# A gated ConvFFN on one core: three plain pairs before the Strassen pairs, the gated activations in smaller DRAM tensors, down loads in program order, one norm chain for the first rows

## The chip, the core and the metric

One core of a Trainium2 chip runs the whole kernel. The metric is the device time in microseconds (us) of one execution, as the median of several runs. Beside it stands one profiled execution, whose trace gives start and duration of the instructions on each engine: PE (TensorE, with PEld for its weight loads), DVE (VectorE), ACT (ScalarE), POOL (GpSimd) and SP (SyncE, here only a queue that issues DMAs).

## The reference

A decoder block on 1024 tokens of width 1024: a mixer (pooling and indexed sparse attention), then a channel mixer, then a last RMSNorm. The change touches only the channel mixer and the last norm:

```python
def conv_ffn(xn, w_up, conv_w, conv_b, w_down):
    h = xn @ w_up                                  # (1024, 1024) @ (1024, 5632)
    h = causal_depthwise_conv3(h, conv_w) + conv_b # over tokens, per channel
    a, b = jnp.split(h, 2, axis=-1)                # 2816 and 2816 channels
    return (jax.nn.silu(a) * b) @ w_down           # (1024, 2816) @ (2816, 1024)

h = h + conv_ffn(rmsnorm(h, norm_ffn_g), w_up, conv_w, conv_b, w_down)
out = rmsnorm(h, norm_final_g)
```

## The kernel before

All large products are taken at near-float32 precision: each operand is split in a high half (a cast to float32r on ACT) and a low half (the difference, on DVE or POOL), and three matmuls of 128x128 by 128x512 are issued for each pair of blocks, high by high, high by low and low by high (`mm3`, lines 85 to 87). A "step" of three such matmuls covers 128 of the contraction.

**Order of the work.** The program is built with a scheduler that keeps dependences and places instructions on each engine by its own model; inside `manual_schedule` the engines named keep program order. PE is in program order in both stages below. A tile pool hands out buffers by tag; when a pool is closed its addresses go to the next pool, and the first use of a buffer waits for the last use of the tiles that lay there.

**Up stage (`ffn_up`).** The normed input lies feature-major in `x2T`, as four blocks X[k, t] (k half of the features, t half of the tokens), X[k, 0] in two 16 KB tiles on the right side of SBUF and X[0, 1], X[1, 1] in the 16 KB tiles `x2T1a` and `x2T1b` on the left. The 5632 columns of `w_up` are taken as 22 pairs c = 0..21: 128 channels of a with the same 128 of b (o = 0, 1). `load(c)` brings the two weight blocks into one of two landing tiles `upr` of tag `raw`. Seven tiles of tag `op` hold split weights.

A plain pair (`plain`, c = 0 only) splits four weight blocks (o, k), the low halves of o = 0 on DVE and of o = 1 on POOL, and makes eight products of 12 matmuls each (96 matmuls), in the order (t, o) = (0,0), (0,1), (1,0), (1,1). A Strassen pair (`pair`, c = 1..21) treats weights and X as 2x2 blocks and makes seven products (84 matmuls), in the order of operands 1, 5, 2, 6, 7, 3, 4. It needs sums of weights (`combined`, on POOL, for c = 1 on DVE) and four sums of X, T1 to T4, each split and kept in a 16 KB tile on the right. They are made once, between the plain pair and pair 1, by 56 DVE operations of 128x512 with 16 ACT casts between; `t2f`, which carries a sum from the first half of that work to the last, takes one of the two landing tiles of tag `raw` while it lives.

`gated(c, H)` then makes the convolution (two operations on DVE for each of a and b, after one on ACT), silu on ACT, the product on POOL, and stores it by POOL's queue to a DRAM tensor `gd`. Accumulators and H have one buffer each.

**Down stage (`ffn_down`).** The product is again one Strassen step over halves of tokens, of the 2816 channels (f) and of the output (d). The 11 blocks of 128 channels in each half are taken in six groups j of two (the last of one). For a group, `prepare_*` loads quarters of `gd` and of `w_down` into landing tiles `raw` (512 KB each), makes sums, and splits them into an operand tile `op` (four of them). The order is: product 1 and 5 (`prepare_1_5`, five loads a group, in the order A(0,0), B(0,0), A(1,0), A(1,1), B(0,1)), then 2, 6 and 7, 3, 4. Each product is 24 matmuls a group. In product 4 the last three groups are kept and run token block by token block, so that rows finish one after the other. `cs`, `ct` keep the sums of products 1 and 5 for later; `h` (tile `hr`) takes the residual by four loads `load_h`.

**Last norm.** `row_done(th, tb, ...)` makes for one block of 128 rows the reciprocal root (`rstd`, ten DVE operations on 128x1), scales the two halves (ACT and DVE) and stores them. It is called for rows 0 to 3 before product 4 and for rows 4 to 7 at the end.

The pools of the down stage: on the right `hr` 32 KB, `gfin` 4 KB, `cs` and `ct` 22 KB each, `u2`, `u4` 8 KB each and small tiles (2.4 KB), where T1 to T4 and X[k, 0] lay before; on the left the four operand tiles (64 KB) and then ten landing tiles (40 KB).

Of the kernel before, what the change touches and what calls it, by code (L numbers as in the profile page):

```python
# [18 lines left out]
P = 128  # L19
D = 1024  # L20
# [19 lines left out]
class K:  # L40
# [4 lines left out]
    def split(self, src, hi, lo, eng=None, first=None):  # L45

        if first:
            first.tensor_copy(hi, src)
        else:
            self.nc.scalar.copy(hi, src)  # L50
        (eng or self.nc.vector).tensor_tensor(lo, src, hi.bitcast(F32), op=ALU.subtract)  # L51

    def rstd(self, pool, ssum, name, n=1, halves=False):


        nc = self.nc
        v, y, t, u = (pool.tile([P, n], F32, tag=f"rs_{c}{n}", name=name + c) for c in "vytu")
        if halves:
            nc.vector.tensor_scalar(v, ssum[:, 0:1], ssum[:, 1:2], EPS, op0=ALU.add, op1=ALU.add)
# [124 lines left out]
    def stages(self):  # L184
# [81 lines left out]
        self.gd = dram("gd", [2, 2, P, NFH, HB])  # L266
# [707 lines left out]
    def ffn_up(self, fw, pool, x2_last, close_h):  # L974
# [23 lines left out]
        def gated(c, H):  # L998
# [12 lines left out]
            nc.gpsimd.dma_start(self.gd[c // NFH, :, :, c % NFH].rearrange("t p c -> p t c"),  # L1011
# [48 lines left out]
        for k in range(4):  # L1060
            f = difference(1, k, xk((0, 1), k), xk((0, 0), k))
            keep(1, k, f)
            less(t2[:, k], xk((1, 1), k), f)
            keep(2, k, t2[:, k])
        for k in range(4):
            keep(3, k, difference(3, k, xk((1, 1), k), xk((0, 1), k)))
        for k in range(4):
            f = pool.tile([P, HB], F32, tag="s4", name=f"tf4_{k}")
            less(f, xk((1, 0), k), t2[:, k])
            keep(4, k, f)  # L1070
        T = {n: [t[:, 0], t[:, 1]] for n, t in T.items()}

        def pair(c):
# [23 lines left out]
            operand_of(4, A[1, 1], nc.gpsimd if c > 1 else nc.vector)  # L1097
# [19 lines left out]
        with self.tc.manual_schedule(engines=PE):  # L1117
            for c in range(1, NF):
                pair(c)

    def ffn_down(self, ring, pool):
# [3 lines left out]
        G, W = self.gd, io["w_down"]  # L1125
        h = pool.tile([P, NB, D], F32, name="hr")
# [4 lines left out]
        groups = [(j, min(2, NFH - j)) for j in range(0, NFH, 2)]  # L1131

        def quarters(j, n):


            def load(src, name):
                t = ring.tile([P, 2, HB], F32, tag="raw", name=f"raw{name}_{j}", bufs=10)[:, 0:n]
                nc.sync.dma_start(t, src[:, j:j + n])
                return t
            return (lambda t, f: load(G[f, t], f"g{t}{f}")), (lambda f, d: load(W[f, d], f"w{f}{d}"))  # L1140

        def operand(p, j, n):
            return ring.tile([P, 4, 2, HB], F32R, tag="op", name=f"op{p}_{j}", bufs=4)[:, :, 0:n]

        def put(t, side, val):
            self.split(val, t[:, 2 * side], t[:, 2 * side + 1])
# [23 lines left out]
        def prepare_6_7(j, n):  # L1170
            A, B = quarters(j, n)
            s, t = cs[:, j:j + n], ct[:, j:j + n]
# [8 lines left out]
        def prepare_3(j, n):  # L1181
            A, B = quarters(j, n)
            p3, a = operand(3, j, n), A(0, 1)
            put(p3, 0, combined(a, a, cs[:, j:j + n], sub))
# [3 lines left out]
        def prepare_4(j, n):  # L1188
            A, B = quarters(j, n)
            p4 = operand(4, j, n)  # L1190
            put(p4, 0, A(1, 1))
            b = B(1, 0)
            put(p4, 1, combined(b, b, ct[:, j:j + n], sub))
            return p4,

# [6 lines left out]
        def run(prepare, pss, fresh, tail=0):  # L1202

            kept = []
            for k, (j, n) in enumerate(groups):
                ts = prepare(j, n)
# [21 lines left out]
        ss = {}  # L1228

        def half_done(th, dh, tb):  # L1230

            b = 4 * th + tb
            if b not in ss:
                ss[b] = pool.tile([P, 2], F32, tag="ss", name=f"ssf{b}", bufs=8)
            junk = pool.tile([P, HB], BF16, tag="junk", name=f"sqf{b}{dh}", bufs=2)
            nc.scalar.activation(junk, quarter(th, dh, tb), AF.Square, scale=D ** -0.5, accum_out=ss[b][:, dh:dh + 1])
# [5 lines left out]
        def row_done(th, tb, scaled):  # L1242

            b = 4 * th + tb
            y = self.rstd(pool, ss[b], f"f{b}", halves=True)
            for dh in (1 - scaled, scaled):
                q, cols = quarter(th, dh, tb), slice(dh * HB, (dh + 1) * HB)
                if dh == scaled:
                    nc.scalar.activation(q, q, AF.Copy, scale=y)
                else:  # L1250
                    nc.vector.scalar_tensor_tensor(q, q, y, gfin[:, cols], op0=ALU.mult, op1=ALU.mult)
                nc.sync.dma_start(io["out"][b * P:(b + 1) * P, cols], q)

        with self.tc.manual_schedule(engines={mybir.EngineType.PE}):
# [35 lines left out]
            for tb in range(4):  # L1290
                q = quarter(0, 1, tb)
                tt(q, y[tb], q, op=add)
                half_done(0, 1, tb)
                row_done(0, tb, 0)
            run(prepare_4, (x,), False, 3)
            for tb in range(4):
# [3 lines left out]
                row_done(1, tb, 1)  # L1300
# [69 lines left out]
```

## Time and profile before

| | |
|---|---|
| median of 3 runs | 1536.83 us (1533.32 to 1537.8) |
| profiled execution, own time | 1532.94 us |
| span of the profiled execution (first to last instruction) | 1530.8 us |
| mean granted TensorE clock, share of full speed | 0.974 |
| PE busy | 1431.6 us, 94% |
| DVE busy | 1177.1 us, 77% |
| ACT, POOL busy | 652.7 us, 491.8 us |

Starts are in us from the start of the span. A row of a timeline gives start, duration, engine, line, operation, output and inputs, shapes and a count; in square brackets, the idle time of the engine before it and what ended it. Durations of pipelined matmuls are modelled, so the distance of their starts is the better measure.

### The profile page before, as it was taken

The numbers are of one execution on the slowest core, as the hardware profiler recorded it, in microseconds if no ns is written. First come the engines' busy times: TensorE is split into PE (matmuls) and PEld (weight loads), VectorE is DVE, ScalarE is ACT, GpSimd is POOL, SyncE is SP. The second block draws the span as 40 slices with busy tenths as digits, with TensorE's granted clock in tenths as the row PEclk, the third lists the DMA queues.
The fourth block names the chain that finished last, engine by engine and source line by source line (L and its number), as shares of the span: only waits on it lengthen the run. The fifth ranks groups of instructions, "written<-read, shape, count | busy, mean of one in ns | idle before, by whom it ended". The sixth has DMA issues, their size and how long they took to land.

```text
span 1530.8 us, 18757 instructions
## 1 busy us (share of the span) xinstructions
PE 1431.6 (94%) x6658; PEld 1173.2 (77%) x6658; DVE 1177.1 (77%) x1960; ACT 652.7 (43%) x1119; POOL 491.8 (32%) x359
## 2 busy tenths in 40 slices
PE   5999999999889899998999499999999997999996
PEld 4888887787678788986887378888888885788885
DVE  7756999999971356878357988888888885859697
ACT  7665322213332456864023434444444443444343
POOL 4102433213433364444100555555555541000000
PEclk9999999999999999999999699999999999999998
DMA  9002422412115466228412022222222215966452
GB/s 339 10 21 86 140 81 100 139 69 62 42 68 194 139 189 181 64 86 267 150 66 103 28 83 83 83 83 83 83 83 83 82 57 192 377 203 210 151 151 110
DMA packets 74062, 184.47 MB, mean 121 GB/s; under 512 B 8560, under 2 KB 13552, under 8 KB 73456
## 3 DMA queue, kind: packets, MB, share of 16 engines
q1 hardware_dynamic: 65360, 159.16, 30.2%
q0 software_dynamic: 8608, 24.12, 4.9%
q8 instruction: 52, 0.85, 0.2%
q14 instruction: 42, 0.34, 0.1%
HBM read 140.25 MB, written 40.89 MB: 118 GB/s over the span
## 4 chain that ended last, share of the span: by engine, by line
PE 64%; DVE 26%; DMA 3%; issue 3%; ACT 3%; POOL 1%; SPq 0%; DVEq 0%; ACTq 0%; POOLq 0%
DVE tk_junk L554 11%; PE up L85 9%; PE up L86 9%; PE up L87 9%; PE d L86 4%; PE d L87 4%; PE d L85 4%; PE o L835 2%; PE pt L818 2%; DVE tk_r L566 2%; DVE tk_cand L567 1%; PE is L439 1%; PE is L440 1%; PE wvp L86 1%; PE wvp L85 1%
## 5 line engine op out<-in xcount | busy, mean ns | idle before, releaser
L554 DVE TENSOR_SCALAR_CACHE_REDUCE tk_junk<-score,tk_cand 128x384 bf16<-128x384 f32 (+1 forms) x186 | 175.0, 941 | 1.8
L85 PE MATMUL up<-T,w 128*128 128x512 f32 x336 | 134.0, 399 | 20.3 <-ACT w L995 20.3
L1005 DVE SCALAR_TENSOR_TENSOR acc<-H,cw,acc 128x1023 f32<-128x1023 f32 x88 | 130.7, 1503 | 15.8 <-ACT acc L1003 14.9
L87 PE MATMUL up<-T,w 128*128 128x512 f32 x336 | 134.0, 399 | 1.1 <-DVE w L996 1.1
L86 PE MATMUL up<-T,w 128*128 128x512 f32 x336 | 133.8, 398 | 0.0
L85 PE MATMUL d<-op 128*128 128x512 f32 x308 | 121.4, 394 | 11.6 <-ACT op L50 11.6
L86 PE MATMUL d<-op 128*128 128x512 f32 x308 | 121.3, 394 | 1.3 <-DVE op L51 1.3
L87 PE MATMUL d<-op 128*128 128x512 f32 x308 | 120.8, 392 | 0.0
L1010 POOL TENSOR_TENSOR acc<-acc,acc 128x1024 f32<-128x1024 f32 x22 | 79.1, 3593 | 120.5 <-ACT w L995 70.8
L995 ACT CAST w<-s 128x512 fp32r<-128x512 f32 x84 | 52.1, 621 | 142.1 <-POOL s L1086 75.7
L996 DVE TENSOR_TENSOR w<-s,w 128x512 fp32r<-128x512 f32 x84 | 104.1, 1240 | 2.2 <-ACT w L995 1.3
L85 PEld LDWEIGHTS up<-T,w 128*128 128x128 f32 x336 | 63.6, 189 | 36.0 <-ACT w L995 20.8
L85 PEld LDWEIGHTS d<-op 128*128 128x128 f32 x308 | 58.5, 190 | 24.5 <-ACT op L50 12.4
L87 PEld LDWEIGHTS up<-T,w 128*128 128x128 f32 x336 | 63.6, 189 | 17.3 <-DVE w L996 1.9
L85 PE MATMUL up<-x2T,w 128*128 128x512 f32 x184 | 74.4, 405 | 2.3 <-ACT w L995 2.3
L86 PEld LDWEIGHTS up<-T,w 128*128 128x128 f32 x336 | 63.7, 190 | 15.2
L87 PE MATMUL up<-x2T,w 128*128 128x512 f32 x184 | 74.1, 403 | 0.0
L86 PE MATMUL up<-x2T,w 128*128 128x512 f32 x184 | 74.1, 402 | 0.0
L825 DVE TENSOR_TENSOR PT<-pt,PT 128x512 fp32r<-128x512 f32 (+3 forms) x96 | 50.5, 554 | 29.9 <-ACT PT L824 29.4
L996 POOL TENSOR_TENSOR w<-upr,w 128x512 fp32r<-128x512 f32 x22 | 34.6, 1574 | 112.5 <-DVE w L996 89.8
L1003 ACT ACTIVATE acc<-H,cb,cw 128x1024 f32<-128x1024 f32 x44 | 54.8, 1246 | 35.6 <-DVE H L1114 24.4
L86 PEld LDWEIGHTS d<-op 128*128 128x128 f32 x308 | 58.6, 190 | 14.4 <-DVE op L51 2.1
(871 smaller groups left out, 4097.4 us busy)
## 6 DMA issues: line engine op xcount, KB each, us to landing
upr<-w_up SPq DMA_DIRECT2D x44, 512.0 KB, 4.1
rawg<-gd SPq DMA_DIRECT2D x40, 512.0 KB, 4.9
raww<-w_down SPq DMA_DIRECT2D x35, 512.0 KB, 4.8
gd<-acc POOLq DMA_DIRECT2D x22, 512.0 KB, 3.2
g<-gt SPq DMA_DIRECT2D x32, 256.0 KB, 2.0
xb<-x SPq DMA_DIRECT2D x8, 512.0 KB, 5.6
xTr<-xT SPq DMA_DIRECT2D x8, 512.0 KB, 6.4
mixd<-mixed SPq DMA_DIRECT2D x16, 256.0 KB, 2.6
```

The costliest lines, as they stand in the source:

```text
L85: t.matmul(ps, sh, mh, start=start, stop=False, skip_group_check=onto)
L86: t.matmul(ps, sh, ml, start=False, stop=False, skip_group_check=onto)
L87: t.matmul(ps, sl, mh, start=False, stop=stop, skip_group_check=onto)
L554: nc.vector.tensor_scalar(junk[:, :W], self.score[b], thr, None, op0=ALU.is_ge, op1=ALU.add, accum_out=cnt[:, j:j + 1])
L566: nc.vector.tensor_scalar(r, cnt, float(TOPK), float(1 << bit), op0=ALU.is_lt, op1=ALU.mult)
L818: nc.tensor.transpose(pt[:, j - j0, :], t[:, j * P:(j + 1) * P], self.ident)
L825: nc.vector.tensor_tensor(PT[:, j0:j1, 1, :], pt[:, 0:j1 - j0, :], PT[:, j0:j1, 0, :].bitcast(F32), op=ALU.subtract)
L995: nc.scalar.copy(t[:, 0], src)
L996: eng.tensor_tensor(t[:, 1], src, t[:, 0].bitcast(F32), op=ALU.subtract)
L1003: nc.scalar.activation(a, H[o], AF.Identity, bias=cb[:, n:n + 1], scale=cw[:, n, 2:3])
L1005: nc.vector.scalar_tensor_tensor(a[:, d:], H[o][:, 0:S - d], cw[:, n, 2 - d:3 - d], a[:, d:], op0=ALU.mult, op1=ALU.add)
L1010: nc.gpsimd.tensor_tensor(b, a, b, op=ALU.mult)
```

## The change

1. `plain` is used for c = 0, 1 and 2, and the Strassen pairs begin with c = 3. The sums T1 and T2 are issued after the weights of pair 1 in program order, T3 and T4 after those of pair 2. Sums of weights are always on POOL.
2. `gd` is split into twelve DRAM tensors, one for each group of two chunks.
3. In the down stage SP is in program order too. There are 8 landing tiles instead of 10. The operand tiles move to the right pool, one tag each, taken in turn, behind `u2`, `u4`, `hr`, `gfin`; `cs`, `ct` become one tile a group in the left pool, and the small tiles go there too.
4. Rows 0 to 3 get one `rstd` on 128x4 (`rows_done`), whose work is issued within product 4, ahead of the preparation of its last three groups; the low half of the first of these is held behind it in program order. Their stores are issued after all loads.

```diff
-        self.gd = dram("gd", [2, 2, P, NFH, HB])
+        self.down_groups = [(j, min(2, NFH - j)) for j in range(0, NFH, 2)]
+        self.gd = {(f, j): dram(f"gd{f}{j}", [2, P, n, HB]) for f in range(2) for j, n in self.down_groups}
...
-        def plain(c):
+        def plain(c, work=None):
...
+            if work:
+                work()
...
-        for k in range(4):
-            f = difference(1, k, xk((0, 1), k), xk((0, 0), k))
...
+        with self.tc.manual_schedule(engines=PE):
+            plain(1, sums_1_2)
+            plain(2, sums_3_4)
...
-                (nc.gpsimd if c > 1 else nc.vector).tensor_tensor(t, a, b, op=op)
+                nc.gpsimd.tensor_tensor(t, a, b, op=op)
...
-            for c in range(1, NF):
+            for c in range(3, NF):
...
+        u2, u4 = (pool.tile([P, 4, HB], F32, name=n) for n in ("u2", "u4"))
         h = pool.tile([P, NB, D], F32, name="hr")
         gfin = pool.tile([P, D], F32, name="gfin")
-        cs, ct = (pool.tile([P, NFH, HB], F32, name=n) for n in ("chs", "cht"))
-        u2, u4 = (pool.tile([P, 4, HB], F32, name=n) for n in ("u2", "u4"))
+        cs, ct = {}, {}
...
-                t = ring.tile([P, 2, HB], F32, tag="raw", name=f"raw{name}_{j}", bufs=10)[:, 0:n]
-                nc.sync.dma_start(t, src[:, j:j + n])
+                t = ring.tile([P, 2, HB], F32, tag="raw", name=f"raw{name}_{j}", bufs=8)[:, 0:n]
+                nc.sync.dma_start(t, src)
...
-            return ring.tile([P, 4, 2, HB], F32R, tag="op", name=f"op{p}_{j}", bufs=4)[:, :, 0:n]
+            tag = f"op{turn[0] % 4}"
+            turn[0] += 1
+            return pool.tile([P, 4, 2, HB], F32R, tag=tag, name=f"op{p}_{j}")[:, :, 0:n]
...
-            s, t = cs[:, j:j + n], ct[:, j:j + n]
+            s, t = cs[j], ct[j] = [ring.tile([P, 2, HB], F32, name=f"{nm}{j}")[:, 0:n] for nm in ("chs", "cht")]
...
-            put(p4, 0, A(1, 1))
+            first = put(p4, 0, A(1, 1))
+            if behind:
+                self.tc.keep_in_program_order(first)
+                behind.clear()
...
+                if work and k == len(groups) - tail:
+                    work()
+                    behind.append(1)
...
-        with self.tc.manual_schedule(engines={mybir.EngineType.PE}):
+        def rows_done(th, tb, n, scaled):
+
+            stores = []
+            y = self.rstd(ring, ss[th][:, tb:tb + n], f"f{th}{tb}", n, halves=True)
+            for i in range(n):
...
+            yield
+            for dst, q in stores:
+                nc.sync.dma_start(dst, q)
...
+        def first_rows():
+            for tb in range(4):
+                q = quarter(0, 1, tb)
+                tt(q, y[tb], q, op=add)
+                half_done(0, 1, tb)
+            next(first_stores)
+
+        with self.tc.manual_schedule(engines={mybir.EngineType.PE, mybir.EngineType.SP}):
...
-                row_done(0, tb, 0)
-            run(prepare_4, (x,), False, 3)
+            run(prepare_4, (x,), False, 3, first_rows)
+            next(first_stores, None)
...
-                row_done(1, tb, 1)
+                for _ in rows_done(1, tb, 1, 1):
+                    pass
```

## Rows read from the trace of the kernel before

**Rows 1.** The page: busy time of the matmuls, one matmul line of the down stage.

```profile
PE 1431.6 (94%) x6658; PEld 1173.2 (77%) x6658; DVE 1177.1 (77%) x1960; ACT 652.7 (43%) x1119; POOL 491.8 (32%) x359
...
L85 PE MATMUL d<-op 128*128 128x512 f32 x308 | 121.4, 394 | 11.6 <-ACT op L50 11.6
```

**Rows 2.** Waits of PE, 780 to 1531 us: total, times, longest.

```profile
PE up L85 <- ACT w L995: 22.7, 2, 20.3
PE d L85 <- ACT op L50: 11.6, 2, 10.7
PE up L85 <- DVE u L1108: 2.5, 1, 2.5
```

**Rows 3.** Timeline of PE, up stage, around pair 1.

```profile
849.68 0.40 PE L85 MATMUL up<-x2T,w 128*128 128x512 f32 x1
...
872.99 0.79 PE L85 MATMUL up<-T,w 128*128 128x512 f32 x1 [20.34 <-ACT w L995]
...
898.61 0.40 PE L85 MATMUL up<-x2T,w 128*128 128x512 f32 x1
...
901.41 0.40 PE L85 MATMUL up<-T,w 128*128 128x512 f32 x1
```

**Rows 4.** Windows: length, busy of five engines, granted clock, DMA share, GB/s.

```profile
870.00:880.00 10.00, 5.87 (x13) 4.19 (x14) 9.97 (x15) 3.50 (x6) 10.00 (x1) 0.50 0.30 105
```

**Rows 5.** Timeline of DVE, first sum of T and the end of them.

```profile
834.21 0.68 DVE L1048 TENSOR_TENSOR tf<-x2T1a,x2T 128x512 f32<-128x512 f32 x1
...
878.34 2.75 DVE L1086 TENSOR_TENSOR s<-upr,s 128x512 f32<-128x512 f32 x1
```

**Rows 6.** Timeline of POOL, the plain pair's low halves and its product.

```profile
824.71 2.97 POOL L996 TENSOR_TENSOR w<-upr,w 128x512 fp32r<-128x512 f32 x2 [89.82 <-DVE w L996]
858.00 22.53 POOL L1010 TENSOR_TENSOR acc<-acc,acc 128x1024 f32<-128x1024 f32 x1 [30.32 <-DVE acc L1005]
```

**Rows 7.** Timeline of SP's queue, up stage: the two loads of pair 1's weights.

```profile
827.71 0.80 SPq L988 DMA_DIRECT2D upr<-w_up  x2
```

**Rows 8.** Timeline of ACT: first cast of pair 1's weights.

```profile
840.87 0.63 ACT L995 CAST w<-upr 128x512 fp32r<-128x512 f32 x1
```

**Rows 9.** Timeline of PE, products 6 and 7 of the last pair, their starts.

```profile
1283.99 0.39 PE L85 MATMUL up<-x2T1b,w 128*128 128x512 f32 x1
...
1286.74 0.40 PE L85 MATMUL up<-T,w 128*128 128x512 f32 x1
```

**Rows 10.** Timeline of SP's queue: the load of the last norm's gain.

```profile
1284.19 0.33 SPq L1263 DMA_DIRECT2D gfin<-norm_final_g  x1
```

**Rows 11.** Timeline of DVE: last pair's convolution.

```profile
1290.83 4.00 DVE L1005 SCALAR_TENSOR_TENSOR acc<-H,cw,acc 128x1022 f32<-128x1022 f32 x3
```

**Rows 12.** Chain of work that ended last, from up stage to down stage: start, us, what.

```profile
1297.59 4.15 DMA gd<-acc
...
1301.87 3.79 DMA rawg<-gd
...
1305.75 1.24 DVE chs L1149
...
1308.15 2.37 DVE op L51 x2
```

**Rows 13.** Waits of SP's queue, 1270 to 1531 us.

```profile
SPq L1138 <- DVE op L51: 105.7, 44, 10.8
```

**Rows 14.** Timeline of PE, kept groups of product 4: first and last matmul.

```profile
1502.50 0.39 PE L85 MATMUL d<-op 128*128 128x512 f32 x1
...
1515.88 0.39 PE L87 MATMUL d<-op 128*128 128x512 f32 x1
```

**Rows 15.** Timeline of DVE: the last low half before the kept groups.

```profile
1499.57 0.70 DVE L51 TENSOR_TENSOR op<-raww,op 128x512 fp32r<-128x512 f32 x1
```

**Rows 16.** Chain of work that ended last, its last rows: start, us, what.

```profile
1523.71 0.75 DVE hr L1251
...
1526.29 0.75 DVE hr L1251
```

More of the change, by code (lines that the diff above doesn't have):

```diff
@@ L1058, in keep, with sums_1_2, sums_3_4 @@
             self.split(f, T[n][:, 0, k], T[n][:, 1, k])
-        for k in range(4):
-            f = difference(1, k, xk((0, 1), k), xk((0, 0), k))
[L1062 to L1070, printed above, removed]
+        def sums_1_2():
+            for k in range(4):
+                f = difference(1, k, xk((0, 1), k), xk((0, 0), k))
+                keep(1, k, f)
+                less(t2[:, k], xk((1, 1), k), f)
+                keep(2, k, t2[:, k])
+        def sums_3_4():
+            for k in range(4):
+                keep(3, k, difference(3, k, xk((1, 1), k), xk((0, 1), k)))
+            for k in range(4):
+                f = pool.tile([P, HB], F32, tag="s4", name=f"tf4_{k}")
+                less(f, xk((1, 0), k), t2[:, k])
+                keep(4, k, f)
+        with self.tc.manual_schedule(engines=PE):
+            plain(1, sums_1_2)
+            plain(2, sums_3_4)
         T = {n: [t[:, 0], t[:, 1]] for n, t in T.items()}
@@ L1125, in ffn_down @@
         G, W = self.gd, io["w_down"]
+        turn = [0]
+        u2, u4 = (pool.tile([P, 4, HB], F32, name=n) for n in ("u2", "u4"))
         h = pool.tile([P, NB, D], F32, name="hr")
         gfin = pool.tile([P, D], F32, name="gfin")
[L1128 to L1129 removed]
+        cs, ct = {}, {}
         add, sub, tt = ALU.add, ALU.subtract, nc.vector.tensor_tensor
[L1131 removed]
+        groups = self.down_groups
         def quarters(j, n):
             def load(src, name):
[L1137 to L1138 removed]
+                t = ring.tile([P, 2, HB], F32, tag="raw", name=f"raw{name}_{j}", bufs=8)[:, 0:n]
+                nc.sync.dma_start(t, src)
                 return t
[L1140 removed]
+            return (lambda t, f: load(G[f, j][t], f"g{t}{f}")), (lambda f, d: load(W[f, d][:, j:j + n], f"w{f}{d}"))
         def operand(p, j, n):
[L1143 removed]
+            tag = f"op{turn[0] % 4}"
+            turn[0] += 1
+            return pool.tile([P, 4, 2, HB], F32R, tag=tag, name=f"op{p}_{j}")[:, :, 0:n]
         def put(t, side, val):
[L1146 removed]
+            return self.split(val, t[:, 2 * side], t[:, 2 * side + 1])
         def combined(dst, a, b, op):
@@ L1183, in prepare_3 @@
             p3, a = operand(3, j, n), A(0, 1)
-            put(p3, 0, combined(a, a, cs[:, j:j + n], sub))
+            put(p3, 0, combined(a, a, cs[j], sub))
             put(p3, 1, B(1, 1))
@@ L1190, in prepare_4 @@
             p4 = operand(4, j, n)
-            put(p4, 0, A(1, 1))
+            first = put(p4, 0, A(1, 1))
+            if behind:
+                self.tc.keep_in_program_order(first)
+                behind.clear()
             b = B(1, 0)
-            put(p4, 1, combined(b, b, ct[:, j:j + n], sub))
+            put(p4, 1, combined(b, b, ct[j], sub))
             return p4,
+        behind = []
         def steps(ps, t, n, tb, fresh, first, last):
@@ L1226, in load_h @@
             nc.sync.dma_start(h[:, 4 * th:4 * th + 4, cols], self.hd[4 * th:4 * th + 4, :, cols].rearrange("b p c -> p b c"))
-        ss = {}
+        ss = [ring.tile([P, 4, 2], F32, name=f"ssf{th}") for th in range(2)]
         def half_done(th, dh, tb):
[L1232 to L1236, printed above, removed]
+            junk = ring.tile([P, HB], BF16, tag="junk", name=f"sqf{th}{tb}{dh}", bufs=2)
+            nc.scalar.activation(junk, quarter(th, dh, tb), AF.Square, scale=D ** -0.5,
+                                 accum_out=ss[th][:, tb, dh:dh + 1])
         def gain(th, dh, tb):
@@ L1240, in gain @@
             tt(q, q, gfin[:, dh * HB:(dh + 1) * HB], op=ALU.mult)
[L1242 to L1252, printed above, removed]
-        with self.tc.manual_schedule(engines={mybir.EngineType.PE}):
+        def rows_done(th, tb, n, scaled):
+            stores = []
+            y = self.rstd(ring, ss[th][:, tb:tb + n], f"f{th}{tb}", n, halves=True)
+            for i in range(n):
+                b = 4 * th + tb + i
+                for dh in (1 - scaled, scaled):
+                    q, cols = quarter(th, dh, tb + i), slice(dh * HB, (dh + 1) * HB)
+                    if dh == scaled:
+                        nc.scalar.activation(q, q, AF.Copy, scale=y[:, i:i + 1])
+                    else:
+                        nc.vector.scalar_tensor_tensor(q, q, y[:, i:i + 1], gfin[:, cols], op0=ALU.mult, op1=ALU.mult)
+                    stores.append((io["out"][b * P:(b + 1) * P, cols], q))
+            yield
+            for dst, q in stores:
+                nc.sync.dma_start(dst, q)
+        first_stores = rows_done(0, 0, 4, 0)
+        def first_rows():
[5 more added lines that the diff above has]
+        with self.tc.manual_schedule(engines={mybir.EngineType.PE, mybir.EngineType.SP}):
             x, y = banks("x", 1), banks("y", 5)
```

17 lines of the change are left out of this document (7 added, 10 removed).

## Prediction

> **What bounds the kernel now.** I read the busy times first: PE is at work for 94% of the span [rows 1], so time is won only where PE stands still or runs at the lower of its two clocks, and lost where it gets more matmuls. Then the waits of PE from the up stage on [rows 2]: three carry nearly all of it, 20.3 and 2.5 us inside the up stage and 10.7 us at the head of the down stage. Then the timelines around each.
>
> *Up stage.* Pair 1 begins at 849.68 and pair 2 at 898.61, 48.93 us for 84 matmuls [rows 3]. The twelve from 898.61 to 901.41 took 2.80 us, so 0.2333 us each and 19.60 us for a pair: 29.3 us are lost. 22.8 are the two waits; the rest is a smaller wait and matmuls at a granted clock of 0.50 (1.2 of 2.4 GHz) after the long one [rows 4]. The wait is for work on DVE: the sums T, from 834.21 until the row at 878.34 [rows 5].
>
> *Down stage.* Pair 21 ends with product 7: it starts at 1286.74 [rows 9], and 12 matmuls at 0.2333 end it at 1289.54. The down stage has 3 x 308 = 924 matmuls [rows 1]. From 1502.50 to 1515.88 there are 60, so 59 steps of 0.2268 us [rows 14]; 924 take 209.6 us and the last ends at 1516.11. From 1289.54 that is 226.6, so 17.0 us are lost, 10.7 of it the first wait. The chain says why: the last chunk's store to `gd` (4.15 us), then the load of A(1,1) of the first group (3.79), which needs chunks 11 and 12 only but reads the tensor that chunk 21 writes, then sum, cast and low halves [rows 12].
>
> *Tail.* From the last matmul at 1516.11 to the end at 1530.8 are 14.7 us, in which DVE goes through a norm chain for each row block, 2.58 us apart at the end [rows 16].
>
> **The change, part by part.** The sum is made on the profiled execution, 1532.94 us (its span plus 2.1 around it); it lies 3.9 below the median of 1536.83, and I take the gain off that median.
>
> *Three plain pairs.* Two pairs get 96 matmuls instead of 84: 24 x 0.2333 = 5.6 us more of PE. The 29.3 us between go if PE is fed meanwhile, so 23.7 at best. T is first needed at 849.68 + 44.8 + 2.8 = 897.3, 19 us after DVE ended the sums [rows 5], so T isn't late next. Late next may be the weights of the new plain pairs. Their landing tile is ready early (loads issued at 827.71 [rows 7]), but their o = 1 low halves stay on POOL. Before, pair 1's cast came at 840.87 [rows 8]; a third one in its place puts POOL's request near 842.5. PE needs this half with the third matmul of its third product, at 849.68 + 24 x 0.2333 + 0.5 = 855.8. Undisturbed it costs 1.5 us (2.97 for two [rows 6]) and is in time: nothing lost. The other bound is the row of POOL's product, which asked at 858.00, in the middle of DVE's sums, and took 22.53 us [rows 6]; it ended at 880.53, and the DVE operation that began at 878.34 took 2.75 us instead of the 0.68 of its shape [rows 5]. So POOL did nothing until DVE paused at 878.3. DVE's work from 834.21 on is about 41 us here (the same 44.1, less three sums and four low halves of pair 1, plus two of the plain pair, at 0.68 at most). If POOL is shut out until 875, PE stands from 855.8 to 876.5, and with 2 us at the lower clock 22.7 of the 23.7 are gone.
>
> Between the two lies what DVE does in order. Pair 2's weights can land only in the tile that pair 1's leave (the other of the two is `t2f`), and that is when POOL has made both low halves. DVE's queue holds two low halves of pair 2 between the sums, so when DVE comes to them it must stop, and there POOL gets in. I put that stop at 857 to 859 (request of POOL, two halves and about 5 us of load as the scheduler counts on them, and casts; an estimate, no row shows it): PE waits about 2 us and then runs some 2 us longer at the lower clock. I take 4 us, near the good bound: 19.7 won, between 1 and 23.7.
>
> A rule bears on this place. The Trainium skill, "SBUF — State Buffer", section "Who interferes with whom", says that DVE with two SBUF inputs and a GpSimd instruction that reads SBUF exclude each other, and that the second to issue waits until the first has finished. By that rule POOL would wait for one DVE operation at most, 0.7 us, the half would be there at 845, and all 23.7 would be won, 4 us more than in my sum. The row of 22.53 us speaks against so short a wait; I keep the rule as a rival.
>
> Sums of weights on POOL always: the line acted for c = 1 alone, now a plain pair, so nothing.
>
> *`gd` in twelve tensors, landing tiles and operands elsewhere.* A(1,1) of the first group no longer waits for the store that lands at 1301.74 [rows 12]. What comes next is where the tiles lie. The right pool before is 98.4 KB, its start 2.4 KB under T1, and `gfin` at 32 to 36 KB crosses from T2 into T3: its load went out at 1284.19, just after T3's product ended at 1283.99 [rows 9, 10]. So pools fill upward in order of creation. After, the right pool is 116 KB over the same 96: `u2` to `gfin` (52 KB) reach over T2, and the first operand tile is exactly T3, free at 1283.99, the second T4, free at 1289.54. On the left two sums (8 KB) and the first landing tile lie in `x2T1a`, unread since the plain pairs, most others in `x2T1b`, whose product ends at 1286.74. So product 1's first loads can be there long before, its casts begin at 1284, and two casts and two low halves (about 1.2 each, half of 2.37 [rows 12]) are done by 1289: PE goes on at 1289.54 without a gap. Product 5 is late next. A(1,1) and B(0,1) go out after 1286.74 and land about 1291 (3.79 [rows 12]), but DVE has the last pair's convolution until 1294.83 [rows 11], which stands ahead. From there sum to second low half took 1305.75 to 1310.52, 4.8 us [rows 12], so product 5 has all operands at 1299.6. Product 1 ends at 1289.54 + 24 x 0.2268 = 1295.0: a wait of 4.6 and some 2 us of lower clock stay. 17.0 - 6.6 = 10.4 won. Bounds: no wait there, 17.0; or product 1 late as well, by the loads' landing and a cast, 5. I take 10.
>
> *SP in program order, 8 landing tiles.* Loads wait for landing tiles already (105.7 us of SP's waits are for DVE to free one [rows 13]) while PE had no stop after the head [rows 2]: hidden, nothing. The loads of `h` move behind the first product's and out of the way of the first quarters; they are needed 100 us later.
>
> *First rows early.* By 1516.11 DVE has then no row but the last block's chain and what is left of the one before: a block costs 2.58 plus an addition of 0.7 [rows 15, 16], 3.3, under the 15 matmuls, 3.4 us, between blocks. After the last matmul: addition and square about 1.5 (two operations of 128x512, estimated from the 0.70 of rows 15), chain and scaling 2.58, last scaling to the end 1530.8 - 1527.04 = 3.8 as before, and up to 1 of the block before: 8 to 9 instead of 14.7, so 6.2 won. Against it, rows 0 to 3 (four scalings of 0.75 [rows 16], a chain of 128x4 of about 2.3) come ahead of the kept groups' halves on DVE, 5.3 us. Those ended at 1500.27 [rows 15]; the third kept group is needed at 1502.50 + 2.7 = 1505.2: 4.9 of cover, so 0.4 or so is seen; with no cover it would be 5.3, below the gain still. I take 5.5, between 2 and 6.2.
>
> *Sum.* 19.7 + 10 + 5.5 = 35.2. 1532.94 becomes 1497.7, the median 1536.83 becomes 1501.6.
>
> **The rivals.**
> *POOL shut out until the sums are done.* For it: the 22.53 us. Against it: DVE's stop at pair 2's halves. It leaves 1 of 23.7: gain 16.5, 1520.
> *POOL gets in at once*, by a pause of DVE that falls right or because it waits for one DVE operation only. For it: the plain pair's own halves took 1.5 us each [rows 6]; against it the same 22.53. 23.7 + 10 + 5.5 = 39.2, or 1498. The rule of the Trainium skill named above would give this case.
> *The loads of `gd` still wait for chunk 21*, so the split doesn't do what it says. Product 1 runs at once, product 5 still at 1308 to 1310.5: about 1 is won instead of 10, 1511. Against it: group 0 and chunk 21 are in different tensors.
> *Slower: SP in program order starves the operands.* Place: SP's queue, where a load that waits for one of 8 tiles holds all behind it, for each of 30 groups of the five products. For it: rows 13. Against it: those waits stood before too, and PE has none behind the head [rows 2]. It decides from 1.3 us of PE wait a group (39.8 / 30): then 35.2 and the 4.6 of a measurable change are eaten, 1541 and more.
>
> **How the numbers follow.** Forecast 0.55, with a range of its own of 1494 to 1510; shut out 0.18; in at once 0.14; `gd` still waited for 0.07; slower 0.06, of which I leave 0.01 within the uncertainty. 0.3%, 4.6 us, is about what a measurement of this kernel can tell from no change. The best of all bounds is 23.7 + 17 + 6.2 = 46.9, 1490; the other end is the shut-out case, 1520, of which half lies beyond. What is outside: half of 0.18, the slower case, a little above and below, under 0.2. Faster 0.93, within 0.3% 0.02, slower 0.05. I name 1501.
>
> **What would show it.** Right: PE's wait of 20.3 us gone, three stretches of 96 matmuls to about 898; POOL's low halves of pair 1 between 842 and 860, at most 3 us of PE wait for them; first matmul of the down stage within 1 us of the last of the up stage, then one wait of 3 to 6 us for product 5; 8 to 9 us from last matmul to end. Wrong: a POOL operation of over 10 us with PE waiting for it near 856; PE waits for `gd`'s store; many short PE waits for casts in the down stage.

## The result, and the profile after

The changed kernel takes 1516.05 us in the median of four runs (1512.42 to 1516.64), the kernel before, on the same chip, 1535.07 (1532.29 to 1537.8): a ratio of 0.9898, 95% interval 0.9869 to 0.9928. That is 19 us (1.2%) faster by the medians and 16 us (1.0%) by the ratio, where 35 were forecast. The sign is right and the size is about half: the time lies above the 1494 to 1510 that the prediction gave its own forecast, within its outer bounds of 1490 to 1520.

Executions differ by up to 11 us in stages that no kernel here changes: over all the profiles the up stage begins between 818.6 and 829.7 us. So the profiles are compared by stage, with four instants: from PE's timeline the start of the first and of the last matmul of the up stage and of the last of the down stage, and the end of the span.

| us | first up | last up | last down | span | up | down | end | sum |
|---|---|---|---|---|---|---|---|---|
| before | 823.65 | 1289.31 | 1515.88 | 1530.8 | 465.7 | 226.6 | 14.9 | 707.1 |
| after | 826.33 | 1279.52 | 1505.02 | 1514.9 | 453.2 | 225.5 | 9.9 | 688.6 |

The page of the changed kernel, busy time of the matmuls:

```profile
PE 1430.4 (94%) x6682; PEld 1173.5 (77%) x6682; DVE 1162.0 (77%) x1909; ACT 649.9 (43%) x1117; POOL 488.5 (32%) x358
```

PE has 24 matmuls more than in [rows 1], as foreseen. Its longest waits from the up stage on:

```profile
PE up L85 <- ACT r L1113: 9.8, 1, 9.8
PE d L85 <- ACT op L50: 5.5, 1, 5.5
PE d L86 <- DVE op L51: 3.3, 1, 3.3
PE d L87 <- DVE op L51: 3.3, 1, 3.3
...
```

Of the waits of [rows 2], those of 20.3 and 2.5 us are gone; one of 9.8 has come in pair 3, two (5.5 and 3.3) stand at the head of the down stage, and one of 3.3 is new before the kept groups. Each is one missed step.

**Pair 3.** Timeline of PE: the pair's start, its second product (the first on a T), its third.

```profile
896.01 0.40 PE L85 MATMUL up<-x2T,w 128*128 128x512 f32 x1
...
898.81 0.40 PE L85 MATMUL up<-T,w 128*128 128x512 f32 x1
...
911.56 0.80 PE L85 MATMUL up<-x2T,w 128*128 128x512 f32 x1 [9.78 <-ACT r L1113]
```

From 826.33 to 896.01 three plain pairs run with no wait over 0.4 us, 69.7 us (288 matmuls at 0.2333 would be 67.2). Then the third product needs the bank from which ACT has yet to copy `r1`. Timeline of ACT:

```profile
876.94 1.24 ACT L1004 ACTIVATE acc<-H,cb,cw 128x1024 f32<-128x1024 f32 x1 [5.97 <-POOL acc L1011]
883.03 0.62 ACT L996 CAST w<-upr 128x512 fp32r<-128x512 f32 x1 [4.84 <-DMA upr<-w_up]
...
908.85 1.06 ACT L1010 ACTIVATE acc<-acc 128x1024 f32<-128x1024 f32 x1 [4.00 <-DVE acc L1006]
909.81 1.22 ACT L1004 ACTIVATE acc<-H,cb,cw 128x1024 f32<-128x1024 f32 x1
910.94 0.56 ACT L1113 COPY r<-up 128x512 f32<-128x512 f32 x1
```

The copy stands behind the third plain pair's gate, which waits for DVE. Timeline of POOL, and of DVE where it stops:

```profile
827.39 4.20 POOL L997 TENSOR_TENSOR w<-upr,w 128x512 fp32r<-128x512 f32 x3 [88.72 <-DVE w L997]
...
844.59 4.98 POOL L997 TENSOR_TENSOR w<-upr,w 128x512 fp32r<-128x512 f32 x1 [13.00 <-ACT w L996]
856.22 1.64 POOL L997 TENSOR_TENSOR w<-upr,w 128x512 fp32r<-128x512 f32 x1 [6.65 <-ACT w L996]
864.55 12.35 POOL L1011 TENSOR_TENSOR acc<-acc,acc 128x1024 f32<-128x1024 f32 x1 [6.70 <-DVE acc L1006]
...
878.02 1.30 POOL L997 TENSOR_TENSOR w<-upr,w 128x512 fp32r<-128x512 f32 x1
...
853.61 0.69 DVE L997 TENSOR_TENSOR w<-upr,w 128x512 fp32r<-128x512 f32 x1 [1.75 <-ACT w L996]
...
856.61 1.79 DVE L1059 TENSOR_TENSOR t2f<-t2f,x2T1b 128x512 f32<-128x512 f32 x1
...
873.97 0.68 DVE L1054 TENSOR_TENSOR tf<-tf,x2T 128x512 f32<-128x512 f32 x1
878.22 2.20 DVE L1006 SCALAR_TENSOR_TENSOR acc<-H,cw,acc 128x1023 f32<-128x1023 f32 x1 [3.57 <-ACT acc L1004]
883.68 0.69 DVE L997 TENSOR_TENSOR w<-upr,w 128x512 fp32r<-128x512 f32 x1 [3.26 <-ACT w L996]
```

and of SP's queue, the loads of pair 3's weights:

```profile
879.35 0.89 SPq L989 DMA_DIRECT2D upr<-w_up  x2
```

Both of POOL's halves of the first new plain pair were in time: the one that the prediction watched, the last of the three from 827.39, was made by 831.6, and PE came to it at 857.4; the other ended at 849.6, and PE came to it at 860.2. POOL's product, asked at 864.55, ended only at 876.90, 2.25 us after DVE's run of sums stopped at 874.65, and the last low half stood behind it. Two things wait for POOL then: the accumulator (ACT's 5.97, DVE's 3.57), and the landing tile, which takes pair 3's weights only at 879.35 (ACT's 4.84, DVE's 3.26). DVE's two stops are 6.8 us; its sums end at 901.4.

**Head of the down stage.** Timelines of SP's queue (the load of B(0,0)), ACT, DVE and POOL around the last pair's gate:

```profile
1262.43 0.33 SPq L1150 DMA_DIRECT2D raww<-w_down  x1
...
1277.96 1.24 ACT L1004 ACTIVATE acc<-H,cb,cw 128x1024 f32<-128x1024 f32 x1 [8.57 <-DVE H L1123]
1281.16 1.24 ACT L1004 ACTIVATE acc<-H,cb,cw 128x1024 f32<-128x1024 f32 x1 [1.96 <-DVE H L1125]
1282.41 1.06 ACT L1010 ACTIVATE acc<-acc 128x1024 f32<-128x1024 f32 x1
1283.37 1.03 ACT L50 CAST op<-rawg 128x1024 fp32r<-128x1024 f32 x1
...
1281.05 3.99 DVE L1006 SCALAR_TENSOR_TENSOR acc<-H,cw,acc 128x1022 f32<-128x1022 f32 x3
1284.96 1.22 DVE L51 TENSOR_TENSOR op<-rawg,op 128x1024 fp32r<-128x1024 f32 x1
1286.09 3.36 DVE L51 TENSOR_TENSOR op<-raww,op 128x1024 fp32r<-128x1024 f32 x1
...
1266.14 2.39 POOL L1011 TENSOR_TENSOR acc<-acc,acc 128x1024 f32<-128x1024 f32 x1 [3.73 <-issue]
...
1285.18 3.18 POOL L1011 TENSOR_TENSOR acc<-acc,acc 128x1024 f32<-128x1024 f32 x1 [15.62 <-DVE acc L1006]
```

Product 1's first cast, at 1283.37, was not late by its load: the load of B(0,0), sent behind that of A(0,0), went out at 1262.43. ACT stood idle for 8.57 us and then had three operations of the gate to do first, DVE four. The second low half took 3.36 us beside POOL's product. Product 5 had no wait. From the last up matmul to the 37th of the down stage 20.9 us pass (1279.52 to 1300.38), 12.5 more than 37 steps of 0.2268; before it was 17.1. The waits are 8.8 of the 12.5, and most of the rest is the lower clock. Windows (length, PE's busy time and matmuls, granted clock, DMA share, GB/s):

```profile
1290.00:1295.00 5.00, 5.00 (x13) 0.50 0.93 304
1295.00:1300.00 5.00, 5.00 (x22) 0.94 0.95 358
```

**Kept groups and end.** Timeline of DVE, and the matmul that waits:

```profile
1485.25 0.68 DVE L51 TENSOR_TENSOR op<-raww,op 128x512 fp32r<-128x512 f32 x1
...
1488.04 2.74 DVE L1273 SCALAR_TENSOR_TENSOR hr<-hr,f00y,gfin 128x512 f32<-128x512 f32 x4
1490.69 1.22 DVE L51 TENSOR_TENSOR op<-rawg,op 128x1024 fp32r<-128x1024 f32 x1
...
1491.96 0.50 PE L87 MATMUL d<-op 128*128 128x512 f32 x1 [3.29 <-DVE op L51]
```

The halves of the second and third kept group are done by 1485.9. The held one, behind the first rows' chain and scalings, belongs to the first kept group, which PE needs first. From the last matmul's start to the end it is 9.9 us instead of 14.9.

### The profile page after: what moved, and what is told of

It is laid out like the page before. It is cut to its first block, busy times and chain, and to the rows that moved or that the text cites. A ratio compares the mean times of both kernels' runs of the same rounds, so it can differ in the third digit from the quotient of the medians.

```text
span 1514.9 us, 18726 instructions
## 1 busy us (share of the span) xinstructions
PE 1430.4 (94%) x6682; PEld 1173.5 (77%) x6682; DVE 1162.0 (77%) x1909; ACT 649.9 (43%) x1117; POOL 488.5 (32%) x358
## 4 chain that ended last, share of the span: by engine, by line
PE 61%; DVE 27%; DMA 4%; issue 3%; ACT 3%; POOL 2%; SPq 0%; DVEq 0%; ACTq 0%; POOLq 0%
DVE tk_junk L555 11%; PE up L85 8%; PE up L87 8%; PE up L86 8%; PE d L86 4%; PE d L87 4%; PE d L85 4%; PE o L836 2%; PE pt L819 2%; DVE tk_r L567 2%; DVE op L51 1%; DVE tk_cand L568 1%; PE is L440 1%; PE is L441 1%; PE wvp L86 1%
## 5 line engine op out<-in xcount | busy, mean ns | idle before, releaser
L1006 DVE SCALAR_TENSOR_TENSOR acc<-H,cw,acc 128x1023 f32<-128x1023 f32 x88 | 133.4, 1533 | 20.5 <-ACT acc L1004 19.7
L85 PE MATMUL up<-T,w 128*128 128x512 f32 x304 | 120.3, 396 | 0.0
L86 PE MATMUL up<-T,w 128*128 128x512 f32 x304 | 120.3, 396 | 0.0
L87 PE MATMUL up<-T,w 128*128 128x512 f32 x304 | 120.2, 396 | 0.0
L1011 POOL TENSOR_TENSOR acc<-acc,acc 128x1024 f32<-128x1024 f32 x22 | 69.8, 3174 | 92.4 <-ACT w L996 63.4
L996 ACT CAST w<-s 128x512 fp32r<-128x512 f32 x76 | 47.2, 621 | 119.6 <-POOL s L1097 73.2
L997 DVE TENSOR_TENSOR w<-s,w 128x512 fp32r<-128x512 f32 x76 | 92.9, 1222 | 1.1 <-ACT w L996 0.2
L85 PE MATMUL up<-x2T,w 128*128 128x512 f32 x200 | 80.9, 405 | 12.1 <-ACT r L1113 9.8
L997 POOL TENSOR_TENSOR w<-upr,w 128x512 fp32r<-128x512 f32 x25 | 41.5, 1665 | 130.1 <-DVE w L997 88.7
L87 PE MATMUL up<-x2T,w 128*128 128x512 f32 x200 | 80.6, 403 | 0.4 <-DVE w L997 0.4
L86 PE MATMUL up<-x2T,w 128*128 128x512 f32 x200 | 80.7, 404 | 0.0
L85 PEld LDWEIGHTS d<-op 128*128 128x128 f32 x308 | 58.6, 190 | 18.2 <-ACT op L50 5.9
L86 PEld LDWEIGHTS d<-op 128*128 128x128 f32 x308 | 58.5, 190 | 16.0 <-DVE op L51 3.8
L87 PEld LDWEIGHTS d<-op 128*128 128x128 f32 x308 | 58.5, 190 | 15.9 <-DVE op L51 3.7
L85 PEld LDWEIGHTS up<-T,w 128*128 128x128 f32 x304 | 57.2, 188 | 13.8
L87 PEld LDWEIGHTS up<-T,w 128*128 128x128 f32 x304 | 57.1, 188 | 13.9
```

What stands on the lines that cost most here:

```text
L85: t.matmul(ps, sh, mh, start=start, stop=False, skip_group_check=onto)
L86: t.matmul(ps, sh, ml, start=False, stop=False, skip_group_check=onto)
L87: t.matmul(ps, sl, mh, start=False, stop=stop, skip_group_check=onto)
L996: nc.scalar.copy(t[:, 0], src)
L997: eng.tensor_tensor(t[:, 1], src, t[:, 0].bitcast(F32), op=ALU.subtract)
L1006: nc.vector.scalar_tensor_tensor(a[:, d:], H[o][:, 0:S - d], cw[:, n, 2 - d:3 - d], a[:, d:], op0=ALU.mult, op1=ALU.add)
```

## Experiments

All are edits of the changed kernel, except where said. Where a wait in the profile decides, there is a single execution and no interval. The table gives the stages as above.

| us | up | down | end | sum | median | ratio to before, 95% |
|---|---|---|---|---|---|---|
| after | 453.2 | 225.5 | 9.9 | 688.6 | 1516.05 | 0.9898 [0.9869, 0.9928] |
| product on DVE | 451.3 | 227.1 | 9.5 | 687.9 | 1511.56 | 0.9867 [0.9837, 0.9898] |
| `r1` first | 453.1 | 227.0 | 9.3 | 689.5 | 1514.74 | 0.9885 [0.9851, 0.9919] |
| low halves on DVE | 444.3 | 226.6 | 9.5 | 680.4 | 1508.61 | 0.9856 [0.9818, 0.9893] |
| last group held | 451.8 | 221.2 | 10.6 | 683.6 | 1512.51 | 0.9865 [0.9828, 0.9901] |
| no taps | 452.4 | 224.3 | 9.5 | 686.2 | 1506.59 | one run |
| one `gd` | 453.7 | 225.7 | 10.1 | 689.5 | 1511.97 | one run |
| small group first | 454.1 | 225.3 | 9.4 | 688.8 | 1519.94 | one run |
| one plain pair | 461.8 | 226.9 | 9.5 | 698.2 | 1527.26 | 0.9973 [0.9954, 0.9993] |
| before, split `gd` | 461.9 | 224.2 | 15.0 | 701.1 | 1525.01 | one run |
| three repairs | 444.3 | 220.8 | 10.0 | 675.1 | 1500.41 | 0.9800 [0.9777, 0.9823] |
| and product | 442.6 | 220.3 | 9.8 | 672.7 | 1501.23 | 0.9815 [0.9793, 0.9837] |
| SP free | 452.3 | 226.9 | 9.3 | 688.5 | 1512.10 | one run |

Among the edits of the changed kernel that leave a stage alone, the up stage took 451.8 to 454.1 us and the down stage 225.5 to 227.1: differences of some 2 us say nothing. Between the two profiles of the old kernel ("before" in the first table, and "before, split `gd`") it is more, 465.7 against 461.9 and 226.6 against 224.2, with nearly the same waits. There the granted clock differs: in the first 5 us of the up stage it was 0.50 (11 matmuls) against 1.00 (19), and some 21 to 26 us after the up stage's last matmul 0.66 (12 matmuls in 5 us) against 1.00 (21). So 6 us between that profile and another may be clock alone. The ratios tell none of the single edits of the first four lines under "after" from the changed kernel, since the intervals overlap; there the stages and the waits are the evidence.

**The first plain pair's product on DVE.**

```diff
-            nc.gpsimd.tensor_tensor(b, a, b, op=ALU.mult)
+            (nc.vector if c == 0 else nc.gpsimd).tensor_tensor(b, a, b, op=ALU.mult)
```

> The product of the first plain pair's gate (line 1011, 12.35 us on POOL in the changed kernel, 10 of them while DVE ran the sums T back to back) goes to DVE, where one 128x1024 costs about 1.2 us. Theory (POOL shut out, its accumulator and the landing tile behind it late, ACT's queue held): ACT's wait of 5.97 us at 876.94 and DVE's two stops of 3.57 and 3.26 us go, the copy of r1 in pair 3 comes about 7 us earlier, TensorE's wait of 9.8 us before that pair's third product falls to 2 to 4 us and the time falls by 7 to 9 us. Rival (DVE is simply full until 905): the wait stays at 9 to 11 us, the time is the same or 1 us longer.

A miss for both: PE's wait fell from 9.8 to 7.9 us, neither to 2 to 4 nor staying at 9 to 11. On POOL's timeline the low half that had stood behind the product is now the one that is shut out:

```profile
864.22 7.87 POOL L997 TENSOR_TENSOR w<-upr,w 128x512 fp32r<-128x512 f32 x1
```

Pair 3's weights are loaded at 872.12 and cast at 875.27, 53.2 us after the up stage began (after: 56.7). DVE still stops for that cast, for 2.76 us.

**The copy of `r1` ahead of the third plain pair's gate on ACT.**

```diff
-            gated(c, H)
+            self.late = [lambda i: late(i, c, H)] if c == 2 else gated(c, H)
...
-            nc.scalar.copy(r1, ps[0])
+            r1c = nc.scalar.copy(r1, ps[0]).ins; self.late and self.late.pop()(r1c)
```

(`late` issues the gate behind the given instruction.)

> The gate of the third plain pair is put behind the copy of r1 of pair 3 in ACT's queue; POOL's 12.35 us stay. Theory that the copy's place in ACT's order costs the wait: the copy comes at 900 to 904 instead of 910.94, TensorE's 9.8 us fall to 1 to 4 us, the time falls by 6 to 9 us. Rival (everything behind DVE's stops is late, so the next operand waits in its place): another wait of 4 to 8 us shows in pair 3 or 4 and the time falls by less than 3 us.

The rival holds. PE's waits now:

```profile
...
PE up L85 <- ACT r L1113: 4.5, 2, 3.8
PE up L85 <- DVE u L1119: 3.8, 1, 3.8
...
```

8.3 us in place of 9.8, and the up stage is no shorter: most of the wait moves to the operands that come next, which are as late.

**Low halves of the plain pairs on DVE.**

```diff
-                    halves(w[o, k], raw[:, o, 4 * k:4 * k + 4], nc.gpsimd if o else nc.vector)
+                    halves(w[o, k], raw[:, o, 4 * k:4 * k + 4], nc.gpsimd if o and c == 0 else nc.vector)
```

> The low halves of plain pairs 1 and 2 that POOL makes (four, 4.98 and 1.64 us among them) go to DVE; POOL keeps the product. If the landing tile that they release is what makes pair 3 late: its load goes out some 8 us earlier and TensorE's 9.8 us shrink by 5 or more. If the product on POOL and ACT's wait behind it are: POOL's product is still over 8 us, the wait in pair 3 stays within 3 us of 9.8, and the time within 4 us. If the full DVE is: the wait grows by the 2.5 us that DVE gets more.

The landing tile, for the most part: pair 3's loads go out at 863.21, 42.3 us after the stage began (after: 53.0), the up stage is 8.9 us shorter, and PE's waits in pair 3 are

```profile
...
PE up L85 <- DVE u L1119: 2.1, 1, 2.1
PE up L85 <- ACT r L1113: 1.0, 1, 1.0
...
```

DVE has 2.5 us more to do and still ends its sums at 888.0, 67.1 us after the stage began (after: 75.1): it stops for weights for 0.63 us only, and not for the accumulator. The product on POOL was not held fixed, though; with DVE's sums placed otherwise it took

```profile
856.33 6.31 POOL L1011 TENSOR_TENSOR acc<-acc,acc 128x1024 f32<-128x1024 f32 x1 [31.36 <-DVE acc L1006]
```

instead of 12.35. What tells the two apart is the pair of runs with the product away: alone, it left a wait of 7.9 us; beside these halves on DVE (last experiment), it made the up stage 1.7 us shorter, no more than profiles differ by. What a product of 12.35 us would cost with the tile early was not tried.

**The last kept group's half is held instead of the first's.**

```diff
-                    behind.append(1)
+                if work and k == len(groups) - 1: behind.append(1)
```

> In the last product the half that is held behind the first rows' work on DVE is the last kept group's, not the first's. Theory (the held half is the one that TensorE needs first): the wait of 3.3 us for it goes, the kept groups begin without a gap, the time falls by 3 to 4 us. Rival (the first rows' chain then slips behind the last rows' additions): the wait goes, but from the last matmul to the end it takes 12 us or more instead of 9.5, and the time is the same.

As the theory has it: the wait of 3.3 us is gone, the down stage is 4.3 us shorter, the end 0.7 longer.

**The last pair's taps left out.** The two earlier taps of the last pair's two convolutions are not computed, so one chunk of g is not the reference's.

```diff
-                for d in (1, 2):
+                for d in (1, 2) if c < NF - 1 else ():
```

> Leaves out the two earlier taps of the last pair's convolution (four DVE operations at line 1006, about 5.2 us), so two chunks of g are not the reference's. Theory for the head of the down stage (product 1's casts and low halves stand behind the last convolution on ACT and DVE): the casts come 1 to 2 us and the low halves 3 to 5 us earlier, TensorE's waits there (5.5 and 3.3 us) fall to 4 and under 1, product 5 waits 0 to 2, and from the last matmul of the up stage to the last of the down stage it takes 220 to 222 us instead of 225.5 to 227.1. Rival (the loads of g and of the weights land late): the first wait stays at 5 to 6 us and the stage at 225 or more.

PE's waits at the head fall to 3.9 and 2.0 us, and to the 37th matmul 9.5 us are lost instead of 12.5. (The other profiles with the head unchanged lose 11.0 to 12.5.) The stage got shorter by less than expected (224.3, not 220 to 222): DVE's first low half now takes 2.55 us beside POOL's product, and the lower clock stays. So part of the two waits, 2.9 of 8.8 us, is the convolution's; that product 1 would start without a gap if nothing of the gate stood ahead was not tried.

**`gd` in one tensor again; and the kernel before with `gd` in twelve.** These two separate the split from the layout. The edit shown is the first one's; the second makes the opposite edit in the kernel before.

```diff
-        self.gd = {(f, j): dram(f"gd{f}{j}", [2, P, n, HB]) for f in range(2) for j, n in self.down_groups}
+        self.gd = dram("gd", [2, 2, P, NFH, HB])
```

> g in one DRAM tensor again, all else as in the changed kernel. Theory (the split is worth what the head gained, about 4.5 us): product 5's sum waits for the last chunk's store and load, TensorE waits 3 to 6 us before product 5, and the down stage takes 229 to 232 us from the last matmul of the up stage to its own last. Rival (the convolution and the casts behind it end later than the store anyway): no wait there and 225.5 to 227 us.

> The kernel before with g in twelve DRAM tensors and nothing else changed. The prediction's step (the load of A(1,1) waits because it reads the tensor that the last chunk's store writes): TensorE's wait of 10.7 us at the head of the down stage falls to 4 to 6 us and the stage from 226.6 to 216 to 222 us. Rival, after the run with one tensor in the new layout showed no wait for the store (the load waits for its landing tile, which lies in the bytes that the last store reads): the wait stays at 10 to 11 us, the load of A(1,1) still goes out 10 us after that of A(1,0), and the stage at 226 to 228.

Both rivals hold in their waits. With one tensor the waits at the head are 5.5 and 3.3 us, those of the changed kernel, and the load of A(1,1) goes out 11.5 us ahead of the last chunk's store, though both use the same tensor:

```profile
1272.05 0.33 SPq L1150 DMA_DIRECT2D rawg<-gd  x1
...
1283.57 0.75 POOL L1013 DMA_DIRECT2D gd<-acc  x1 [0.30 <-POOL acc L1011]
```

With twelve tensors in the old layout PE waits 10.3 us, and SP's queue holds the second of the loads A(1,0), A(1,1) as long as before (10.82), still for the last chunk's store:

```profile
1285.75 10.45 SPq L1138 DMA_DIRECT2D rawg<-gd  x2
```

The stage, 224.2, is under the rival's 226 to 228, but by the granted clock named above. Splitting the tensor does nothing; the new layout took the wait for the store away (the order of SP's queue has a run of its own below). That it was the landing tile of A(1,1) lying over the accumulator that this store reads is argued from the layout, not tried alone.

PE's own first wait in the old layout hung on neither. It ended with product 1's operands, A(0,0) and B(0,0). In the kernel before, A(0,0) was sent when the up stage's last product had ended, and ACT waited for it to land:

```profile
1289.77 0.33 SPq L1138 DMA_DIRECT2D rawg<-gd  x1
...
1298.08 1.04 ACT L50 CAST op<-rawg 128x1024 fp32r<-128x1024 f32 x1 [4.83 <-DMA rawg<-gd]
```

The load behind the store fed product 5, for which PE then waited under 1 us at a time. So the expectation of 4 to 6 us was not a test of the store: both loads had to come earlier, and it is with the new layout that both did.

**The group of one chunk first.**

```diff
-        self.down_groups = [(j, min(2, NFH - j)) for j in range(0, NFH, 2)]
+        self.down_groups = [(0, 1)] + [(j, 2) for j in range(1, NFH, 2)]
```

> The group of one chunk is the first of the down stage instead of the last, so the operands of product 1 and product 5 that stand at the head have half the width: casts 0.6 instead of 1.05 us, low halves 0.68 instead of 1.22. Theory (the head is a chain of ACT and DVE work behind the last convolution): the first wait falls by 0.5, the second from 3.3 to under 2, and the stage by 2 to 4 us. Rival (product 1 has half the matmuls, 2.8 us, and no longer covers product 5's operands): a wait of 2 to 3 us before product 5 and no gain.

A miss: waits of 4.6 and 3.1 us, none before product 5, the stage at 225.3. Half the width halves the casts, but the second low half still takes 2.83 us beside POOL's product.

**One plain pair.** Pairs from c = 1 on, the sums behind plain pair 0, as in the kernel before.

> The plain pairs undone: one of them, sums T behind it, weight sums of pair 1 on DVE, all else as in the changed kernel. By the profiles of before and after the plain pairs are worth 12.5 us, so this kernel takes 1526 to 1530 us and shows TensorE's wait of 20 us for the sums again. If the gain lay elsewhere (the other layout, the order of loads): under 1520.

As expected, 1527.26 us with the wait of 20.3 back: by the ratios' difference (0.9973 to 0.9898) the plain pairs are worth 0.75% or 11.5 us, give or take some 5 us (an estimate from the two intervals), by the stages 8.6; all other parts together are worth 0.27%, 4 us (0.07 to 0.46%).

**SP's queue left to the scheduler in the down stage.**

```diff
-        with self.tc.manual_schedule(engines={mybir.EngineType.PE, mybir.EngineType.SP}):
+        with self.tc.manual_schedule(engines={mybir.EngineType.PE}):
```

> The changed kernel with SP's queue in the down stage left to the scheduler, which puts the loads of h and of the final gain between those of the second group. Theory (the head's gain comes from where the tiles lie, SP's program order costs and wins nothing): the waits at the head stay 5.5 and 3.3 us, no wait of 1 us follows for the second group, and the stage takes 225 to 227 us. Rival (the order keeps 4 MB of h out of the first groups' way): a wait of 1 to 4 us with the second or third group and 228 to 231 us.

The same waits (5.5, 3.3, 3.5) and the same sum. SP's order costs and wins nothing.

**The three repairs together.** Low halves on DVE, last group held, the last pair's product on DVE (`c == NF - 1` in the first edit); then also the first plain pair's product.

> The changed kernel with three repairs: the plain pairs' four low halves on DVE, the hold on the last kept group, the product of the last pair's gate on DVE. If the repairs add: 8.9 us in the up stage, 3.6 in the tail and 1 to 2 at the head by the runs that had them singly, so 13 to 15 us under the changed kernel, 1500 to 1503 us and a ratio of about 0.981 to the kernel before. If DVE's extra work costs elsewhere: under 8 us.

> As the run before, and the product of the first plain pair's gate on DVE too, so that POOL has no operation during the sums. If POOL's 6.3 us of waiting there are still on the path: 1 to 3 us less than without. If not, the time is the same or DVE's 1.2 us more cost up to 1 us.

The first two repairs add: up stage and down stage are 8.9 and 4.7 us shorter, as with each alone (8.9 and 4.3). The third was priced at 1 to 2 us and had not been run by itself; the second wait at the head fell by 0.8 us and the stage is not to be told from that of "last group held". In all 1500.41 us, 2.0% under the kernel before, the best kernel of this study, and its interval lies clear of the changed kernel's. PE's waits in it:

```profile
PE d L85 <- ACT op L50: 5.5, 1, 5.5
PE d L86 <- DVE op L51: 2.5, 1, 2.5
PE up L85 <- ACT w L996: 2.3, 1, 2.3
PE up L85 <- DVE u L1119: 2.1, 1, 2.1
PE up L85 <- ACT r L1113: 1.0, 1, 1.0
...
```

The second product on DVE is not to be told from none: the intervals overlap, and the stages' 2.4 us are within what executions differ by.

## Why the prediction was right in sign and wrong in size

**Plain pairs, 19.7 forecast, 12.5 on the two profiles** (8.6 against the kernel with one plain pair, 461.8 to 453.2; most of what lies between is the granted clock in the profile before). The mechanism held: PE is fed while T is made, T is not late, POOL is shut out for long stretches of DVE's sums. The step that failed is "Late next may be the weights of the new plain pairs": it followed POOL to its first low half, priced PE's wait for it at 4 us with the clock behind it (it was none: the half was made by 831.6), and stopped there. DVE's first stop for weights came at 851.86 to 853.61 and not at the 857 to 859 that the prediction put it at. POOL's next requests were the ones shut out, and what they hold is not PE's next operand but the landing tile of the pair after, and behind that DVE's and ACT's queues: a wait of 9.8 us in pair 3 and some 2 us of lower clock after it (granted clock 0.50 from 910 to 915), which the sum had at nothing. With these halves on DVE the up stage is 17.5 us shorter than with one plain pair (21.4 on the profile before): about the forecast gain was there to be had.

**Head, 10 forecast, 4.6 measured** (17.1 to 12.5; 14.8 in the old layout with split `gd`, so 2.3 with the faster clock there). "Product 1's first loads can be there long before" is right, and the layout is why. "Its casts begin at 1284, and two casts and two low halves are done by 1289" failed: the same convolution that the prediction put ahead of product 5 stands ahead of product 1 on ACT and DVE, and POOL's product behind it adds 2 us to a low half. The casts came 3.9 us after the up stage's last matmul began, not 5.5 before its end, and product 1 waited 5.5 and 3.3 us where the sum had nothing. Product 5, priced at 4.6 of wait, had none: by then product 1 was late by more. And the reason given for the old wait, that A(1,1) reads the tensor that chunk 21 writes, was wrong twice: the store was not waited for on account of the tensor, and the first wait, 10.7 us, was for A(0,0) and B(0,0). The chain of waits [rows 12] names the store that a load came after, not what of the store it needed.

**First rows early, 5.5 forecast; measured, 5.0 at the end less some 4 before the kept groups.** The end fell from 14.9 to 9.9, near the 6.2. "4.9 of cover, so 0.4 or so is seen" failed: the cover was reckoned to the third kept group, but the half that is held is the first's, which has none. The prediction's own bound without cover, 5.3, is the nearer one.

**SP in program order, nothing; weight sums on POOL, nothing.** Right, the first by a run of its own; the second was not tried alone.

The shut-out rival comes nearest with its 1520, but its place was another: PE did not stand at 855.8 but from 901.8, in pair 3. The rival by which POOL gets in at once is out as a rule for this place: three of POOL's operations took 4.98, 12.35 and (in the first experiment) 7.87 us, though the one at 856.22 took 1.64. The sum of the three terms as measured is 12.5 + 4.6 + 5.0 - 4 = 18; the two profiles differ by 18.5 (707.1 to 688.6). Against the other profile of the old layout (701.1) it is 12.5, and by the ratio of the runs some 16.

## What to carry to other kernels

When an engine starves, follow each of its queued operations to what it releases (a landing tile, an accumulator), not only to the operand that the bottleneck needs next. When work is put ahead in a queue, ask of every item behind it, in the order in which it will be needed: the convolution that was seen ahead of product 5 stood ahead of product 1 too, and the held half was the first one wanted. A load that waits for a store need not wait for the tensor; one run with only the tensor split, and one with only the layout changed, tell the two apart. And see first which load the bottleneck's own wait ended on.

## What the runs showed of the hardware

A GpSimd operation on two SBUF tensors can stay without a turn while VectorE issues tensor-tensor operations on SBUF back to back: sixteen of them began after the product had asked at 864.55, and it ended 2.25 us after the last of them did, at 874.65; undisturbed, at 1266.14, that shape took 2.39. At 1285.18 it got in behind a single one, and then the next DVE operation took 3.36 us instead of 1.22. So did the low half at 856.22, and DVE's operation from 856.61 took 1.79 us instead of 0.68. The Trainium skill, "SBUF — State Buffer", section "Who interferes with whom", has the two block each other, the second to issue until the first has finished; the rows at 856 and 1285 agree, those at 864 and of the low half in the first experiment (7.87 us) don't. What lets GpSimd in behind one operation here and not behind sixteen there is open.
